# A feed-forward kernel whose second projection changes from eight block products to seven for most pairs of tiles, with the blocks of tokens in another order

## The chip, the cores and the metric

One Trainium2 chip, one of its cores. The metric is the device time of one execution in microseconds (us), as the median of the runs shown. The engines are named as the profile names them: PE is TensorE's matrix multiply and PEld its weight load, DVE is VectorE, ACT is ScalarE, POOL is GpSimd, SP is SyncE, which issues most of the DMAs.

## The reference, cut to what matters

One layer of a streaming encoder for 2048 frames of a new stream and 64 frames of a running one. A token mixer comes first (windowed attention and a spatial gate), then a normalisation, and then the part that the change is about:

```python
def _post(x, mix, ln1_g, ln1_b, w_gate_up, w_down, ln2_g, ln2_b):
    h = _layernorm(ALPHA * x + mix, ln1_g, ln1_b)
    gu = h @ w_gate_up
    f = (jax.nn.silu(gu[..., :D_FF]) * gu[..., D_FF:]) @ w_down
    return _layernorm(ALPHA * h + f, ln2_g, ln2_b)
```

The model width is 1024 and `D_FF` is 2816, which is 22 tiles of 128 features. Everything is float32.

## The kernel before

**Precision.** A float32 product is made of three matmuls in the type `fp32r`. `split` makes a high part (a copy on ACT, line 108) and a low part (a subtraction on DVE, or on POOL where the caller says so, line 109) of each operand, and PE multiplies high by high, high by low and low by high.

**Stages.** The token mixer comes first. Then `m2_load`, `m2_split`, `m2_mm`, `m2_add`, `m2_ln` and `m2_T` make the hidden rows of each tile of 128 tokens and store them, transposed, in DRAM (`h_d`). Tile 16 holds the 64 frames of the running stream. The feed-forward part goes over four blocks of tokens, of 512, 512, 512 and 576 tokens (`TB`), so the last block has five tiles.

**First projection.** For each block `b` and each of the 22 feature tiles `i`, `product(b, i, p)` makes seven products `p` in place of eight (a scheme of Winograd's kind). Each is 12 matmuls with half of the block's tokens as columns (256, or 288 in the last block). Products 1, 6, 7 and 4 collect in a PSUM bank A, 2 in B, 5 and 3 in C. ACT copies the partial sums out of A (line 859), DVE adds them up (lines 863, 866 and 877), ACT applies the silu (lines 881 and 888), and `out` multiplies and splits the result `f` of half a block (`sh`) into the tile `ff`. The order on PE is 1 of tile i, 4 and 3 of tile i-1, then 5, 6, 2, 7 of tile i, which makes 14 products for a pair of feature tiles.

**Second projection.** `down(b, c, t, h)` is one unit: six matmuls of 512 columns that multiply the pair `c` of feature tiles (2c and 2c+1) of token tile `t` by half `h` of the columns of `w_down`. DVE then adds the PSUM bank to the running sum `y` (line 1218). A pair has eight units in a block of four token tiles. The weights are loaded by SP into `draw` (line 1200, three buffers) and split into `wd` (five buffers).

**Order.** Each engine works through its instructions in the order in which the code issues them, and that order is written by hand. `order` lists the products. The main loop issues, for each position in it, the weights' forms that are due five positions later (`make`), then the product with all its work on ACT, DVE and POOL, and then what `todo` holds for that position: weight splits and units. The positions of a pair are counted from `p0`, the position of product 3 of its second feature tile. On a block's last pair the rows are finished (`finish_steps`), and the last block ends in `z_mm` and what follows, which take its last four feature tiles at once.

Of the kernel before, what the change touches and what calls it, by code (L numbers as in the profile page):

```python
# [43 lines left out]
def hybrid_step(ctx: ExitStack, tc: tile.TileContext, x_prompt, x_sample, xT_prompt, xT_sample, cache_kT, cache_v, w_in,  # L44
# [616 lines left out]
    def m2_T(t):  # L661
# [3 lines left out]
        if t == NT - 1:  # L665
            hT = f1.tile([P, KD, DEC], F32, name="hT", tag="hraw", bufs=4)
        for h in range(2):
            pt = ps1.tile([P, 4, P], F32, name="hTp", tag="pj")
            for j in range(4):
                k = 4 * h + j  # L670
                nc.tensor.transpose(pt[:, j, :m], tt[:m, k * P:(k + 1) * P], ident[:m, :m])
            nc.scalar.activation(hT[:, 4 * h:4 * h + 4, :m], pt[:, :, :m], AF.Copy, scale=1.0 / ALPHA)
        b = min(t // 4, NB - 1)
        o = (t - 4 * b) * P
        nc.scalar.dma_start(out=h_d[b][:, :, o:o + m], in_=hT[:, :, :m])
# [159 lines left out]
    ff, acc, part = {}, {}, {}  # L835
# [6 lines left out]
    def product(b, i, prod):  # L842
        n = TB[b] // 2
        w, h = wf.pop((b, i, prod)), forms[b, prod]
        bank = {1: "A", 6: "A", 7: "A", 4: "A", 2: "B", 5: "C", 3: "C"}[prod]
# [293 lines left out]
    m2_mm(13, 1)  # L1139
    m2_add(13, 1)  # L1140
    m2_T(12)
    m2_mm(13, 0)
    m2_add(13, 0)
    m2_ln(13)
    m2_load(15)
    m2_split(15)
    sums(0, 0)
    m2_mm(14, 0)
    m2_mm(14, 1)
    m2_load(16)  # L1150
    m2_split(16)
    m2_add(14, 1)
    m2_add(14, 0)
    m2_ln(14)
    m2_mm(15, 0)
    m2_T(13)
    m2_add(15, 0)
# [7 lines left out]
    m2_T(14)
    m2_add(16, 0)
    m2_mm(16, 1)
    m2_add(16, 1)
    m2_ln(16)
# [8 lines left out]
    m2_T(16)  # L1178
# [30 lines left out]
    def down(b, c, t, h, last=False):  # L1209

        m, o = rows(t), (t - 4 * b) * P
        units[0] += 1
        on_x = units[0] % 3 == 0
        pd = ps1.tile([P, 512], F32, name="pd", tag="x" if on_x else "pj", bufs=6 if on_x else 2)
        mm3(pd[:m], [((ff[b, i][:, 0, o:o + m], ff[b, i][:, 1, o:o + m]), (wd[b, i, h][:, 0], wd[b, i, h][:, 1]))
                     for i in (2 * c, 2 * c + 1)])
# [263 lines left out]
```

## Time and profile before

| what | value |
|---|---|
| median of 3 runs | 2186.51 us (2185.06 to 2187.17) |
| the profiled execution: time | 2185.13 us |
| the profiled execution: span | 2183.3 us |
| granted TensorE clock, mean | 0.989 |
| PE busy | 2109.5 us, 97% of the span |
| DVE busy | 1484.2 us, 68% |
| ACT busy | 943.1 us, 43% |
| POOL busy | 570.5 us, 26% |

The span runs from the first to the last instruction of the profiled execution; its time is 1.8 us longer. Busy times are averages over stages that differ: the token mixer and the normalisation take about the first 700 us, the four blocks of the feed-forward part the rest. Matmuls are pipelined and the profile's duration of one reaches into the next, so the cost of a matmul is read from the distance between starts.

### The profile page before, as it was taken

What the parts mean: (1) busy time and instruction counts of PE and PEld (TensorE: products, weight loads), DVE (VectorE), ACT (ScalarE), POOL (GpSimd) and SP (SyncE); (2) the same over time, 40 slices, a digit from 0 to 9 for tenths busy, and PEclk for the clock granted to TensorE, in tenths of its full rate; (3) what the DMA queues carried; (4) which work ended last, traced back from release to release, by engine and by line L of the source; (5) the groups of instructions that cost most, each with busy time, mean ns of one, the idle gap of its engine ahead of it and who ended that gap; (6) DMA issues with size and microseconds to landing.
All of it is one profiled execution on the core that took longest, in us unless ns stands there. A gap on an engine that the chain in (4) does not pass through costs nothing.

```text
span 2183.3 us, 35663 instructions
## 1 busy us (share of the span) xinstructions
PE 2109.5 (97%) x13219; PEld 1890.2 (87%) x13219; DVE 1484.2 (68%) x2899; ACT 943.1 (43%) x2255; POOL 570.5 (26%) x508
## 2 busy tenths in 40 slices
PE   8999999989998899999999999999999999999998
PEld 6888888867877899999989999989999998999996
DVE  6877777786788787887765555675555576444446
ACT  6666666663343444444433333433333343333333
POOL 0222222231122556665212221121221121111110
PEclk9999999989999899999999999999999999999999
DMA  5111111042664776777777677786777777555552
GB/s 198 39 40 39 40 39 39 27 161 102 206 215 155 281 248 240 286 251 254 279 260 250 233 258 235 264 288 194 273 248 230 239 260 241 191 191 188 192 194 92
DMA packets 172942, 418.27 MB, mean 192 GB/s; under 512 B 20800, under 2 KB 51264, under 8 KB 172768
## 3 DMA queue, kind: packets, MB, share of 16 engines
q1 hardware_dynamic: 152240, 397.31, 53.2%
q10 hardware_dynamic: 20352, 18.35, 2.5%
q8 instruction: 104, 1.70, 0.3%
q14 instruction: 70, 0.57, 0.1%
q0 software_dynamic: 176, 0.33, 0.1%
HBM read 328.31 MB, written 87.62 MB: 191 GB/s over the span
## 4 chain that ended last, share of the span: by engine, by line
PE 76%; DVE 14%; ACT 4%; issue 3%; DMA 2%; POOL 1%; SPq 0%; ACTq 0%; DVEq 0%; POOLq 0%
PE accA L853 7%; PE accA L855 7%; PE accA L854 7%; PE pd L154 7%; PE pd L155 7%; PE pd L156 7%; PE accC L854 4%; PE accC L853 4%; PE accC L855 4%; PE pj L156 2%; PE pj L155 2%; PE pj L154 2%; PE po L154 2%; PE po L156 2%; PE po L155 2%
## 5 line engine op out<-in xcount | busy, mean ns | idle before, releaser
L109 POOL TENSOR_TENSOR wf<-guraw,wf 128x512 fp32r<-128x512 f32 x173 | 249.3, 1441 | 812.0 <-ACT wf L108 742.4
L853 PE MATMUL accA<-hf,wf 128*128 128x256 f32 (+1 forms) x1408 | 407.6, 290 | 17.5 <-ACT a L859 14.6
L855 PE MATMUL accA<-hf,wf 128*128 128x256 f32 (+1 forms) x1408 | 404.9, 288 | 0.8 <-DVE wf L109 0.8
L854 PE MATMUL accA<-hf,wf 128*128 128x256 f32 (+1 forms) x1408 | 402.7, 286 | 0.0
L1218 DVE TENSOR_TENSOR y<-pd,y 128x512 f32<-128x512 f32 (+1 forms) x354 | 242.9, 686 | 163.0 <-PE pd L156 161.5
L853 PEld LDWEIGHTS accA<-hf,wf 128*128 128x128 f32 x1408 | 266.7, 189 | 29.5 <-ACT a L859 18.5
L154 PE MATMUL pd<-wd,ff 128*128 128x512 f32 (+1 forms) x708 | 280.9, 397 | 0.0
L155 PE MATMUL pd<-wd,ff 128*128 128x512 f32 (+1 forms) x708 | 280.5, 396 | 0.0
L156 PE MATMUL pd<-wd,ff 128*128 128x512 f32 (+1 forms) x708 | 279.4, 395 | 0.0
L854 PEld LDWEIGHTS accA<-hf,wf 128*128 128x128 f32 x1408 | 267.9, 190 | 8.1
L855 PEld LDWEIGHTS accA<-hf,wf 128*128 128x128 f32 x1408 | 266.7, 189 | 1.3 <-DVE wf L109 1.3
L109 DVE TENSOR_TENSOR wd<-draw,wd 128x512 fp32r<-128x512 f32 x176 | 172.4, 980 | 53.2 <-ACT wd L108 47.7
L854 PE MATMUL accC<-hf,wf 128*128 128x256 f32 (+1 forms) x704 | 201.8, 287 | 2.1 <-DVE hf L109 2.1
L853 PE MATMUL accC<-hf,wf 128*128 128x256 f32 (+1 forms) x704 | 203.5, 289 | 0.3 <-ACT hf L108 0.3
L859 ACT COPY a<-accA 128x256 f32<-128x256 f32 (+1 forms) x264 | 99.6, 377 | 239.7 <-PE accA L855 237.3
L855 PE MATMUL accC<-hf,wf 128*128 128x256 f32 (+1 forms) x704 | 202.4, 288 | 0.0
L108 ACT CAST ff<-a 128x256 fp32r<-128x256 f32 (+1 forms) x176 | 72.7, 413 | 292.8 <-DVE a L866 288.2
L108 ACT CAST wf<-guraw 128x512 fp32r<-128x512 f32 x264 | 163.2, 618 | 8.6 <-PE po L156 2.9
L156 PEld LDWEIGHTS pd<-wd,ff 128*128 128x128 f32 (+1 forms) x708 | 131.7, 186 | 33.7
L154 PEld LDWEIGHTS pd<-wd,ff 128*128 128x128 f32 (+1 forms) x708 | 131.9, 186 | 18.1
L155 PEld LDWEIGHTS pd<-wd,ff 128*128 128x128 f32 (+1 forms) x708 | 132.1, 187 | 16.3
L109 DVE TENSOR_TENSOR ff<-a,ff 128x256 fp32r<-128x256 f32 (+1 forms) x176 | 88.4, 502 | 84.6 <-ACT ff L108 84.6
(275 smaller groups left out, 4816.8 us busy)
## 6 DMA issues: line engine op xcount, KB each, us to landing
wf<-wf_d SPq DMA_DIRECT2D x264, 512.0 KB, 4.6
guraw<-in_w_gate_up_dram SPq DMA_DIRECT2D x110, 512.0 KB, 6.3
wf_d<-wf SPq DMA_DIRECT2D x88, 512.0 KB, 5.1
draw<-in_w_down_dram SPq DMA_DIRECT2D x176, 256.0 KB, 4.8
guraw<-in_w_gate_up_dram SPq DMA_DIRECT2D x66, 256.0 KB, 6.5
hraw<-h_d SPq DMA_DIRECT2D x36, 256.0 KB, 5.6
x<-in_xT_prompt_dram SPq DMA_DIRECT2D x32, 256.0 KB, 3.1
catx<-cat_d SPq DMA_DIRECT2D x16, 512.0 KB, 3.7
```

Source lines behind the costliest of these rows:

```text
L108: nc.scalar.copy(hi, src)
L109: (on or nc.vector).tensor_tensor(out=lo, in0=src, in1=hi.bitcast(F32), op=ALU.subtract)
L154: nc.tensor.matmul(out, ah, bh, start=(i == 0), stop=False)
L155: nc.tensor.matmul(out, ah, bl, start=False, stop=False)
L156: nc.tensor.matmul(out, al, bh, start=False, stop=(i == n - 1))
L853: nc.tensor.matmul(ps, wh, hh, start=(new and k == 0), stop=False, skip_group_check=not new)
L854: nc.tensor.matmul(ps, wh, hl, start=False, stop=False, skip_group_check=not new)
L855: nc.tensor.matmul(ps, wl, hh, start=False, stop=(k == 3), skip_group_check=not new)
L859: nc.scalar.copy(part[i, key][:, :n], ps)
L1218: nc.vector.tensor_tensor(out=y, in0=pd[:m], in1=y, op=ALU.add)
```

## The change

1. The block of 576 tokens is now the first block (`TB`, `TILES`), and the order of the tiles in the stage before follows it (`TSEQ`): 0, 1, 2, 3, 16, 4, and so on to 15. The last tile's transposed rows go out in two halves.
2. While the first block runs, POOL makes four sums of quarter blocks of `w_down` for each pair (`w_sum`, 44 in all), and SP stores them in DRAM (`w_store` to `wt_d`).
3. In blocks 1, 2 and 3, the pairs that `strassen(b, i)` names (2 to 9 in blocks 1 and 2, 2 to 8 in block 3, 23 pairs together) use seven products of two units each in place of eight units. A unit is now three matmuls of 512 columns and one addition to `y` on DVE. The seven weights are loaded and split one by one (`load_f`, `split_f`), and seven forms of `f` are split: three directly from the products (`put_f`), four from sums that POOL makes (`f_sums`).
4. In blocks 1 to 3 the PSUM banks have fixed roles (`bank`): A0, A1, C0, C1, S1 (which also holds product 2 of the first projection), S0, D0, D1.
5. The positions of loads, splits and units are set anew, and the last block now ends on four tiles.

```diff
-TB = (512, 512, 512, 576)
-NHX = TB[-1] // 2
-TILES = tuple(tuple(range(4 * b, 4 * b + (5 if b == NB - 1 else 4))) for b in range(NB))
+TB = (576, 512, 512, 512)
+NHX = TB[0] // 2
+TILES = tuple(tuple(range(4 * b, 4 * b + 4)) + ((NP,) if b == 0 else ()) for b in range(NB))
+
+TSEQ = sum(TILES, ())
...
-        if t == NT - 1:
-            hT = f1.tile([P, KD, DEC], F32, name="hT", tag="hraw", bufs=4)
+        if t == TSEQ[-1]:
+            hT = [f1.tile([P, 4, P], F32, name="hT", tag="hraw", bufs=4) for _ in range(2)]
...
+    def bank(name):
+
+        if name not in banks:
+            banks[name] = ps1.tile([P, 512], F32, name=f"bank{name}", **({"tag": "pj"} if name[0] == "D" else {"tag": "x", "bufs": 6}))
+        return banks[name]
+
+    def half_form():
+
+        if not spare:
+            f = f2.tile([P, 4 * NHX], F32R, name="ff", tag="ff", bufs=4)
+            spare.extend(f[:, j * 2 * NHX:j * 2 * NHX + 512].rearrange("p (s t) -> p s t", s=2) for j in range(2))
+        return spare.pop(0)
...
+    def strassen(b, i):
+
+        return b > 0 and 1 < i // 2 < NFF // 2 - (2 if b == NB - 1 else 1)
+
+    def put_f(b, c, prod, src):
+        f = ffs[b, c, prod] = half_form()
+        split(f[:, 0], f[:, 1], src)
+
+    def f_sums(b, c):
+
+        x, y = g_t.pop((b, 2 * c)), g_t.pop((b, 2 * c + 1))
+        for prod, o, a, d, op in ((5, y[:, 1], x[:, 1], y[:, 1], ALU.add), (7, x[:, 1], x[:, 0], x[:, 1], ALU.subtract),
+                                  (6, x[:, 0], y[:, 1], x[:, 0], ALU.subtract), (3, y[:, 0], y[:, 0], x[:, 0], ALU.subtract)):
+            nc.gpsimd.tensor_tensor(out=o, in0=a, in1=d, op=op)
+        for prod, o in ((5, y[:, 1]), (6, x[:, 0]), (7, x[:, 1]), (3, y[:, 0])):
+            put_f(b, c, prod, o)
...
+            acc[i, bk] = (bank({"A": f"A{i % 2}", "C": f"C{i % 2}", "B": "S1"}[bk]) if b else
+                          ps1.tile([P, 512], F32, name=f"acc{bk}", tag="x", bufs=6))
...
         def out(sh, g, u):
+            if strassen(b, i):
+                if sh == 0:
+                    g_t[b, i] = f2.tile([P, 4, P], F32, name="g", tag="wsum", bufs=3).rearrange("p (s a) q -> p s (a q)", s=2)
+                to = g_t[b, i][:, sh]
+                nc.vector.tensor_tensor(out=to, in0=u, in1=g, op=ALU.mult)
+
+                if not (sh and i % 2 == 0):
+                    put_f(b, i // 2, 4 if sh else 1 + i % 2, to)
+                if sh and i % 2:
+                    f_sums(b, i // 2)
+                return
             nc.vector.tensor_tensor(out=g, in0=u, in1=g, op=ALU.mult)
...
+    def w_sum(c, j):
+
+        i0, i1 = 2 * c, 2 * c + 1
+        out, x, y = (((i0, 0), (i0, 1), (i0, 0)), ((i0, 1), (i1, 1), (i0, 1)), ((i1, 1), (i1, 1), (i0, 0)),
+                     ((i1, 0), (i1, 0), (i1, 1)))[j]
+        nc.gpsimd.tensor_tensor(out=w_kept[out], in0=w_kept[x], in1=w_kept[y], op=ALU.subtract)
+
+    def w_store(c, j):
+        nc.sync.dma_start(out=wt_d[c][:, j], in_=w_kept[((2 * c, 0), (2 * c, 1), (2 * c + 1, 1), (2 * c + 1, 0))[j]])
...
+    def unit(b, c, prod, u):
+        pd = bank({1: f"D{u}", 6: f"D{u}", 7: f"D{u}", 4: f"D{u}", 2: "S0"}.get(prod, f"S{1 - u}"))
+        f, w = ffs[b, c, prod], wd[b, c, "f", prod]
+        new = prod in (1, 2, 5)
+        fh, fl = f[:, 0, u * P:u * P + P], f[:, 1, u * P:u * P + P]
+        nc.tensor.matmul(pd, fh, w[:, 0], start=new, stop=False, skip_group_check=not new)
+        nc.tensor.matmul(pd, fh, w[:, 1], start=False, stop=False, skip_group_check=not new)
+        nc.tensor.matmul(pd, fl, w[:, 0], start=False, stop=True, skip_group_check=not new)
+        r, h = Y_OF[prod]
+        y = y_t[TILES[b][2 * r + u]][:, h * 512:(h + 1) * 512]
+        nc.vector.tensor_tensor(out=y, in0=pd, in1=y, op=ALU.add)
...
+            if strassen(b, 2 * c):
+                for prod, q0, q1 in ((1, -7, -3), (2, -6, -2), (6, -2, 2), (5, -1, 3), (3, 1, 5), (7, 3, 7), (4, 5, 9)):
+                    at(p0 + q0, lambda b=b, c=c, prod=prod: load_f(b, c, prod))
+                    at(p0 + q1, lambda b=b, c=c, prod=prod: split_f(b, c, prod))
+                for q, prod, u in ((0, 1, 0), (1, 2, 0), (2, 1, 1), (3, 2, 1), (5, 6, 0), (6, 5, 0), (7, 5, 1), (8, 3, 0), (8, 6, 1),
+                                   (9, 3, 1), (10, 7, 0), (11, 7, 1), (12, 4, 0), (13, 4, 1)):
+                    at(p0 + q, lambda b=b, c=c, prod=prod, u=u: unit(b, c, prod, u))
+                continue
+            if b == 0:
+                d_load, d_split = (-6, -2, 8, 0), (1, 0, 10, 3)
+                for j, q0, q1 in ((0, 2, 4), (1, 4, 6), (2, 5, 7), (3, 11, 13)):
+                    at(p0 + q0, lambda c=c, j=j: w_sum(c, j))
+                    at(p0 + q1, lambda c=c, j=j: w_store(c, j))
...
-                where = (2, 3, 4, 5, 7, 8, 9, 10, 12, 13) if last else (2, 4, 5, 7, 9, 10, 12, 13)
+                where = (5, 6, 7, 8, 9, 12, 13, 14, 15, 16) if b == 0 else (2, 4, 5, 7, 9, 10, 12, 13)
                 if c == 0 and b:
-                    where = (6, 10, 12, 14, 15, 16, 17, 18, 19, 20) if last else (6, 10, 12, 14, 15, 16, 17, 18)
-                elif c == 1 and last:
-                    where = (3, 4, 5, 6, 7, 9, 10, 11, 12, 13)
+                    where = (10, 12, 14, 16, 17, 18, 19, 19) if b == 1 else (6, 10, 12, 14, 15, 16, 17, 18)
...
-    for k in range(5):
+    for k in range(4):
```

## Rows read from the trace of the kernel before

**Rows 1.** The page, busy time, share of the span and instructions of each engine.
```profile
PE 2109.5 (97%) x13219; PEld 1890.2 (87%) x13219; DVE 1484.2 (68%) x2899; ACT 943.1 (43%) x2255; POOL 570.5 (26%) x508
```

**Rows 2.** Busy time of each engine by stretch, then granted clock, DMA share, GB/s.
```profile
700.00:750.00 50.00, 41.60 (x272) 38.10 (x271) 37.06 (x46) 20.73 (x44) 24.43 (x17) 0.86 0.83 296
...
900.00:1000.00 100.00, 100.00 (x694) 93.23 (x694) 80.53 (x116) 46.27 (x102) 60.93 (x43) 1.00 0.70 249
...
1300.00:1400.00 100.00, 100.00 (x689) 92.96 (x687) 53.22 (x92) 34.82 (x79) 15.91 (x12) 1.00 0.69 232
```

**Rows 3.** Waits of PE from 740 us on: total, times, longest.
```profile
PE accA L853 <- ACT a L859: 13.2, 13, 2.8
```

**Rows 4.** PE's instructions in order of time, a pair in block 2.
```profile
1301.44 0.40 PE L154 MATMUL pd<-wd,ff 128*128 128x512 f32 x1
...
1302.84 0.28 PE L853 MATMUL accB<-hf,wf 128*128 128x256 f32 x1
...
1304.28 0.40 PE L154 MATMUL pd<-wd,ff 128*128 128x512 f32 x1
...
1334.20 0.28 PE L853 MATMUL accB<-hf,wf 128*128 128x256 f32 x1
```

**Rows 5.** DVE's instructions in order of time, the same pair.
```profile
1304.48 0.42 DVE L863 TENSOR_TENSOR a<-accB,a 128x256 f32<-128x256 f32 x1 [0.75 <-PE accB L855]
...
1315.36 0.41 DVE L863 TENSOR_TENSOR a<-accC,a 128x256 f32<-128x256 f32 x1
1316.25 0.43 DVE L866 TENSOR_TENSOR a<-a,a 128x256 f32<-128x256 f32 x1 [0.48 <-ACT a L888]
1317.15 0.43 DVE L109 TENSOR_TENSOR ff<-a,ff 128x256 fp32r<-128x256 f32 x1 [0.47 <-ACT ff L108]
```

**Rows 6.** ACT's instructions in order of time, the copy in front of that last row.
```profile
1316.71 0.41 ACT L108 CAST ff<-a 128x256 fp32r<-128x256 f32 x1 [0.49 <-DVE a L866]
```

**Rows 7.** POOL's groups of instructions by shape: count, busy, mean ns.
```profile
L109 POOL TENSOR_TENSOR xl<-x,xh 128x256 fp32r<-128x256 f32 x2 | 1.5, 729 | 0.0
```

**Rows 8.** Timeline of block 0, DVE and POOL instructions.
```profile
904.10 0.68 DVE L109 TENSOR_TENSOR wf<-wsum,wf 128x512 fp32r<-128x512 f32 x1
904.71 0.68 DVE L1218 TENSOR_TENSOR y<-pd,y 128x512 f32<-128x512 f32 x1
904.86 1.29 POOL L809 TENSOR_TENSOR wsum<-guraw 128x512 f32<-128x512 f32 x1 [1.57 <-DVE wf L109]
```

**Rows 9.** PE, the end of a unit in block 2.
```profile
1329.68 0.40 PE L156 MATMUL pd<-wd,ff 128*128 128x512 f32 x1
1329.92 0.28 PE L853 MATMUL accC<-hf,wf 128*128 128x256 f32 x1
```

**Rows 10.** DVE, the same moments.
```profile
1329.63 0.69 DVE L866 TENSOR_TENSOR a<-a,a 128x256 f32<-128x256 f32 x1 [0.48 <-ACT a L888]
1330.79 0.42 DVE L109 TENSOR_TENSOR ff<-a,ff 128x256 fp32r<-128x256 f32 x1 [0.47 <-ACT ff L108]
1331.13 0.68 DVE L1218 TENSOR_TENSOR y<-pd,y 128x512 f32<-128x512 f32 x1
```

**Rows 11.** A DVE and a POOL instruction that overlap in block 2.
```profile
1313.58 1.30 POOL L109 TENSOR_TENSOR wf<-guraw,wf 128x512 fp32r<-128x512 f32 x1 [3.48 <-ACT wf L108]
...
1313.61 1.83 DVE L109 TENSOR_TENSOR wd<-draw,wd 128x512 fp32r<-128x512 f32 x1
```

**Rows 12.** A wait of PE for DVE at a block's start.
```profile
1067.21 0.68 DVE L109 TENSOR_TENSOR hf<-hraw,hf 128x512 fp32r<-128x512 f32 x1
...
1067.94 0.39 PE L854 MATMUL accC<-hf,wf 128*128 128x256 f32 x1 [0.49 <-DVE hf L109]
```

**Rows 13.** PE's long waits at two block boundaries.
```profile
1451.78 0.39 PE L853 MATMUL accA<-hf,wf 128*128 128x256 f32 x1 [2.84 <-ACT a L859]
...
1805.72 0.40 PE L853 MATMUL accA<-hf,wf 128*128 128x288 f32 x1 [2.26 <-ACT a L859]
```

**Rows 14.** Stretches after those two waits; third column from the right: granted clock.
```profile
1454.00:1455.00 1.00, 1.00 (x4) 0.81 (x3) 1.00 (x1) 0.00 (x0) 0.85 (x1) 0.50 1.01 414
...
1805.00:1810.00 5.00, 4.28 (x28) 4.03 (x29) 4.94 (x7) 1.49 (x4) 3.25 (x2) 1.00 0.98 380
```

**Rows 15.** DMAs of `draw` in blocks 1 to 3, from issue to landing.
```profile
DMA to landing us min/median/max: 2.7/5.2/9.6
```

More of the change, by code (lines that the diff above doesn't have):

```diff
@@ L69, in hybrid_step @@
     hy_d = [dram.tile([P, D], F32, name=f"hy_d{t}") for t in range(NT)]
+    wt_d = [dram.tile([P, 4, 512], F32, name=f"wt_d{c}") for c in range(NFF // 2)]
     hs_d = [{p: dram.tile([P, 4, TB[b] // 2], F32, name=f"hs_d{b}_{p}") for p in (4, 5, 6, 7)} for b in range(NB)]
@@ L664, in m2_T @@
         hT = cat_t[t][:, 0].rearrange("p (k q) -> p k q", q=P)
-        if t == NT - 1:
-            hT = f1.tile([P, KD, DEC], F32, name="hT", tag="hraw", bufs=4)
+        if t == TSEQ[-1]:
+            hT = [f1.tile([P, 4, P], F32, name="hT", tag="hraw", bufs=4) for _ in range(2)]
+        b = next(i for i in range(NB) if t in TILES[i])
+        o = TILES[b].index(t) * P
         for h in range(2):
@@ L671, in m2_T @@
                 nc.tensor.transpose(pt[:, j, :m], tt[:m, k * P:(k + 1) * P], ident[:m, :m])
[L672 to L675, printed above, removed]
+            half = hT[h] if t == TSEQ[-1] else hT[:, 4 * h:4 * h + 4]
+            nc.scalar.activation(half[:, :, :m], pt[:, :, :m], AF.Copy, scale=1.0 / ALPHA)
+            if t == TSEQ[-1]:
+                nc.scalar.dma_start(out=h_d[b][:, 4 * h:4 * h + 4, o:o + m], in_=half[:, :, :m])
+        if t != TSEQ[-1]:
+            nc.scalar.dma_start(out=h_d[b][:, :, o:o + m], in_=hT[:, :, :m])
         nc.scalar.dma_start(out=hy_d[t][:m], in_=tt[:m])
@@ L833, in form, with ff_tile @@
             nc.gpsimd.tensor_tensor(out=src, in0=gu_src[b, i][2], in1=src, op=ALU.subtract)
-    ff, acc, part = {}, {}, {}
+    ff, acc, part, banks = {}, {}, {}, {}
+    ffs, spare, g_t = {}, [], {}
+    def bank(name):
[7 more added lines that the diff above has]
+        return spare.pop(0)
+    def ff_tile(b, i, k):
+        m = rows(TILES[b][k])
+        if b == 0:
+            return tuple(ff[b, i][:, s_, k * P:k * P + m] for s_ in range(2))
+        return tuple(ff[b, i, k // 2][:, s_, k % 2 * P:k % 2 * P + m] for s_ in range(2))
+    def strassen(b, i):
[10 more added lines that the diff above has]
+            put_f(b, c, prod, o)
     def tmp(name):
@@ L1138, in hybrid_step @@
     sources(0, 1)
[L1139 to L1146, printed above, removed]
-    sums(0, 0)
[L1148 to L1157, printed above, removed]
+    m2_mm(TSEQ[13], 1)
+    m2_add(TSEQ[13], 1)
+    m2_T(TSEQ[12])
+    m2_mm(TSEQ[13], 0)
+    m2_add(TSEQ[13], 0)
+    m2_ln(TSEQ[13])
+    m2_load(TSEQ[15])
+    m2_split(TSEQ[15])
+    sums(0, 0)
+    m2_mm(TSEQ[14], 0)
+    m2_mm(TSEQ[14], 1)
+    m2_load(TSEQ[16])
+    m2_split(TSEQ[16])
+    m2_add(TSEQ[14], 1)
+    m2_add(TSEQ[14], 0)
+    m2_ln(TSEQ[14])
+    m2_mm(TSEQ[15], 0)
+    m2_T(TSEQ[13])
+    m2_add(TSEQ[15], 0)
     make(2)
-    m2_mm(15, 1)
-    m2_add(15, 1)
-    m2_ln(15)
+    m2_mm(TSEQ[15], 1)
+    m2_add(TSEQ[15], 1)
+    m2_ln(TSEQ[15])
     make(3)
-    m2_mm(16, 0)
+    m2_mm(TSEQ[16], 0)
     make(EARLY - 1)
[L1165 to L1169, printed above, removed]
+    m2_T(TSEQ[14])
+    m2_add(TSEQ[16], 0)
+    m2_mm(TSEQ[16], 1)
+    m2_add(TSEQ[16], 1)
+    m2_ln(TSEQ[16])
     store_forms(0)
     product(*order[0])
-    m2_T(15)
+    m2_T(TSEQ[15])
     sums(0, 1, (5, 6))
@@ L1177, in hybrid_step @@
     prep.pop(0)()
-    m2_T(16)
+    m2_T(TSEQ[16])
     product(*order[3])
@@ L1209, in down @@
     def down(b, c, t, h, last=False):
-        m, o = rows(t), (t - 4 * b) * P
+        m, k = rows(t), TILES[b].index(t)
         units[0] += 1
[L1213 to L1216, printed above, removed]
+        if b:
+            pd = bank(("D0", "D1", "S0")[units[0] % 3])
+        else:
+            on_x = units[0] % 3 == 0 and c < NFF // 2 - 1
+            pd = ps1.tile([P, 512], F32, name="pd", tag="x" if on_x else "pj", bufs=6 if on_x else 2)
+        mm3(pd[:m], [(ff_tile(b, i, k), (wd[b, i, h][:, 0], wd[b, i, h][:, 1])) for i in (2 * c, 2 * c + 1)])
         y = y_t[t][:m, h * 512:(h + 1) * 512]
@@ L1333, in hybrid_step @@
     NO = len(order) // NB
-    for t in TILES[0]:
-        at(6 + t, lambda t=t: new_y(t))
+    for k, t in enumerate(TILES[0]):
+        at(6 + k, lambda t=t: new_y(t))
     for b in range(NB):
```

89 lines of the change are left out of this document (54 added, 35 removed).

## The prediction

> **What bounds the kernel now.** First the page's busy times: PE is busy 97% of the span, DVE 68%, POOL 26% [rows 1]. These are averages, so next the same columns by stretch. From 900 to 1000 us (block 0) and from 1300 to 1400 us (block 2) PE is busy all 100 us at the full clock, with DVE at 80.5 and 53.2 us; from 700 to 750 us, where the feed-forward part begins, PE is busy 41.6 of 50 us and the clock is 0.86 [rows 2]. The waits say the same: from 740 us on PE waits 13.2 us for ACT's copies, in 13 pieces [rows 3], which lie at the block boundaries, and next to nothing inside a block. So inside a block PE sets the time, and a matmul saved there is time saved, unless something else becomes late.
>
> **What a matmul costs.** The timeline of PE shows a unit's six matmuls from 1301.44 to 1302.84, so 1.40 us, 0.233 us each, and a product's twelve to 1304.28, so 1.44 us; from one product 2 to that of the next pair it is 1334.20 - 1302.84 = 31.36 us [rows 4]. That is 14 x 1.44 + 8 x 1.40 = 31.36: no idle time at all.
>
> **Matmuls removed.** A changed pair has 7 products x 2 units x 3 = 42 matmuls of 512 columns in place of 8 x 6 = 48. Six fewer give 6 x 0.233 = 1.40 us, and 23 pairs 32.2 us. The 576-token block changes places, which leaves all other counts as they are.
>
> **Work added in a changed pair.** DVE gets 14 additions to y in place of 8, and three more low parts each of f and of the weights. A 512-column instruction takes 0.68 us and hands DVE on after 0.61 [rows 8], so a 256-column one of 0.42 hands it on after about 0.34. That is 9 x 0.61 + 3 x 0.34 = 6.5 us, on top of 0.532 x 31.36 = 16.7 us: 23.2 of about 31 us, 75%. Block 0 ran DVE at 80.5% without a wait of PE [rows 2], so the load alone costs nothing. ACT gets six short copies (34.8% busy now), POOL four additions of 128x256, SP three more loads. What matters is the order on DVE.
>
> **The new chain.** At p0, `product` issues product 3, then `f_sums`, and only then does `todo` issue the first units. DVE's queue then reads: add product 3, multiply, low part of form 4, low parts of forms 5, 6, 7 and 3 (each waits for POOL and ACT), addition of unit (1,0), low part of the weights for product 4, addition of unit (2,0). Unit (2,1) uses the same bank S0 as (2,0), so PE can't start it before that last addition is done. DVE does wait in order: at 1329.92 a unit was done [rows 9], DVE sat idle 0.47 us for ACT, did the low part at 1330.79, and only then, at 1331.13, the addition of that unit [rows 10].
>
> From T, the end of product 3's matmuls:
> - DVE's addition starts 0.20 later (1304.28 to 1304.48) [rows 4, 5]. The multiplication starts 0.89 after that, the low part of form 4 0.90 later again and takes 0.43 [rows 5]: T + 2.42.
> - POOL starts 0.08 after DVE's result (904.78 to 904.86) [rows 8]. An addition of 128x256 takes 0.73 [rows 7]; four of them, one after the other, with 0.03 of overlap, take 2.83: T + 5.33.
> - ACT's copy starts some 0.05 later, and DVE's low part 0.44 after the copy's start (1316.71 to 1317.15) [rows 5, 6]: T + 5.82.
> - That low part hands DVE on after 0.34, the addition of (1,0) after 0.61, the weights' low part after 0.61, and the addition of (2,0) takes 0.68: T + 8.06. PE follows 0.05 after DVE (1067.89 to 1067.94) [rows 12]: T + 8.11.
>
> PE itself would be there after unit, product 5, unit, product 6, unit, product 2: 3 x 0.70 + 3 x 1.44 = T + 6.42. It waits 1.69 us.
>
> Collisions add to it. A DVE instruction with two inputs in SBUF that meets a POOL instruction waits for it: 1.83 us in place of 0.68, ending 0.56 after POOL's end [rows 11]. The low parts of forms 5 and 6 meet POOL's additions so; I allow 0.1 to 0.2 us and take 1.75 us for the wait. Its lower bound is 1.4 (POOL at 0.65), its upper bound 2.6 (each collision delays POOL by a whole low part). Per pair the change then saves 1.40 and loses 1.75; 23 x 1.75 = 40.3 us, bounds 32 to 60.
>
> A rule of the Trainium skill speaks against this part: the GPSIMD Engine Reference, section Engine selection, keeps two-input elementwise work off GpSimd, as about two times slower than VectorE. By that an addition would take an estimated 0.84 us in place of the row's 0.73 [rows 7], and the sum would come out 23 x 4 x 0.11 = 10 us higher.
>
> **Block 0.** POOL makes 44 more sums of 128x512 at 1.29 us [rows 8], 5.2 us per pair. There it is busy 60.9% of 31.36 us = 19.1 us [rows 2], so 24.3 us of a pair that grows longer (ten units and wider products): hidden, by a five-position lead of the forms. If that cover went, a pair would lose one sum, 1.3 us. The stores and loads of SP cost nothing while a load's four-position lead (4 x 2.24 = 9 us) covers its landing, 5.2 us at the median and 9.6 at most [rows 15].
>
> **The first stage and the boundaries.** Block 0's forms and products get 12.5% wider in the stretch where PE already idles [rows 2]: of 37 us of DVE time there perhaps a third scales, 37 x 0.33 x 0.125 = 1.5 us, the wider last tile adds about 0.5, and the fifth tile's finishing at the first boundary about 1. I take +3 us. Tile 16 now comes fifth, so its load follows close behind the store of its rows by the mixer; its split comes a loop step later, which hides it. Fixed banks and new positions could also close some of the 13.2 us of waits [rows 3], so the bounds are -6 and +12.
>
> **The sum.** 2185.1 (the profiled execution's time: 2183.3 of span and 1.8 around it) - 32.2 + 40.3 + 3 = 2196.2 us. The profiled execution lies 1.4 us below the median of the runs, well within the 0.2% (4.4 us) that a measurement of this kernel can tell from no change.
>
> **The rivals.**
> - *Most likely, 0.50:* the wait at unit (2,1), 1.4 to 2.4 us in each changed pair: 2187 to 2212, 2196 taken. 0.40 of it is slower, 0.10 within the bound.
> - *Faster, 0.20:* the wait isn't there, because DVE comes to the additions in time. What speaks for it is DVE's and ACT's free time; what speaks against it is the order [rows 9, 10]. It decides where the wait falls under (32.2 - 3)/23 = 1.27 us. With none: 2185.1 - 32.2 + 3 = 2156.
> - *A shorter chain, 0.12:* POOL and DVE hand over faster than rows of other shapes say, wait about 1.0 us: 2185.1 - 32.2 + 23 + 3 = 2179; half of it faster, half within the bound.
> - *Slow sums on POOL, 0.08:* additions that take twice DVE's 0.42 us [rows 5], so 0.84 us, make the chain 0.44 us longer in each pair: 2196 + 10 = 2206. The Trainium skill's section on engine selection, above, has it so.
> - *The clock, 0.05:* after PE's wait of 2.84 us at a boundary the granted clock fell to 0.50, its lower level of 1.2 GHz; after one of 2.26 us it stayed at 1.00 [rows 13, 14]. Some 3.4 us at half the rate lose 1.7 us. If the new wait came near 2.8 us in every pair, the time would be about 2185 - 32 + 23 x (2.8 + 1.7) + 3 = 2260. [...]
> - *Late weights, 0.05:* seven loads in place of four raise the DMA share (0.69 in block 2) [rows 2]. A load that lands at 9.6 us instead of 5.2 is 0.6 us late, and ACT, DVE and PE wait: up to 23 x 0.6 = 14 us more, 2210.
>
> **The numbers.** Faster: 0.20 + 0.06 = 0.26. Within the bound: 0.10 + 0.06 = 0.16. Slower: 0.40 + 0.08 + 0.05 + 0.05 = 0.58. The range goes from 2158, which leaves out about half of the case without a wait, to 2220, which takes in slow sums and late weights and leaves out the clock and the upper end of the wait. Of the likeliest case alone it is 2187 to 2212.
>
> **What would show it.** Right: in the middle of blocks 1 to 3, PE waits once per pair, 1.4 to 2.4 us, at the second unit of product 2, put down to DVE's addition to y; DVE idles for ACT or POOL just before its additions; a pair takes 31.4 to 32.4 us where eight units took 31.36; block 0 takes about 36.7 us per pair (14 products of 1.44 x 1.125 us and 10 units of 1.40) with no waits. Wrong: a pair of 29.96 us with PE fully busy (the faster rival), half-clock stretches inside blocks (the clock), PE waiting for weight splits behind a DMA (late weights), or waits in block 0 behind POOL's sums.

## The result and the profile after

The changed kernel takes 2257.93 us (median of 4, 2257.21 to 2258.49), the kernel before 2186.10 us beside it; the ratio is 1.0328, with a 95% interval of 1.031 to 1.0346. It is slower by 3.3%, outside the predicted range of 2158 to 2220 us.

The page of the changed kernel, its span and the busy times, answers to [rows 1]:
```profile
span 2256.3 us, 36282 instructions
...
PE 2111.6 (94%) x13081; PEld 1887.1 (84%) x13081; DVE 1613.2 (71%) x3176; ACT 1001.6 (44%) x2385; POOL 697.8 (31%) x644
```
138 matmuls fewer (23 x 6) than in [rows 1], yet PE is busy 2.1 us longer. So besides waits something makes PE work more slowly. The waits of PE from 700 us on, total, times and longest, show the first part:
```profile
PE bankS L1321 <- DVE y L1326: 58.1, 25, 5.7
PE bankA L900 <- ACT a L906: 14.8, 8, 4.7
...
PE bankS L900 <- DVE y L1326: 2.9, 4, 1.2
```
Nothing like the first row is in [rows 3]. L1321 is the first matmul of `unit`, L1326 its addition to y. It is the wait that the prediction put at unit (2,1), in each of the 23 pairs. One of them, in the last block, on DVE, then POOL, then PE; the number in brackets is the idle time ahead of an instruction and what ended it:
```profile
2037.20 0.42 DVE L910 TENSOR_TENSOR a<-bankC,a 128x256 f32<-128x256 f32 x1 [0.20 <-PE bankC L902]
2038.11 0.43 DVE L917 TENSOR_TENSOR g<-a,a 128x256 f32<-128x256 f32 x1 [0.48 <-ACT a L949]
2039.01 0.42 DVE L113 TENSOR_TENSOR ff<-g,ff 128x256 fp32r<-128x256 f32 x1 [0.47 <-ACT ff L112]
2040.72 0.63 DVE L113 TENSOR_TENSOR ff<-g,ff 128x256 fp32r<-128x256 f32 x1 [1.29 <-ACT ff L112]
2042.43 1.30 DVE L113 TENSOR_TENSOR ff<-g,ff 128x256 fp32r<-128x256 f32 x3 [1.08 <-ACT ff L112]
2043.66 0.68 DVE L1326 TENSOR_TENSOR y<-bankD,y 128x512 f32<-128x512 f32 x1
2044.26 0.68 DVE L113 TENSOR_TENSOR wf<-guraw,wf 128x512 fp32r<-128x512 f32 x1
2044.86 0.68 DVE L1326 TENSOR_TENSOR y<-bankS,y 128x512 f32<-128x512 f32 x1
```
```profile
2039.52 3.27 POOL L879 TENSOR_TENSOR g<-g 128x256 f32<-128x256 f32 x4 [1.69 <-DVE ff L113]
...
2039.52 0.74 POOL L879 TENSOR_TENSOR g<-g 128x256 f32<-128x256 f32 x1 [1.69 <-DVE ff L113]
2040.33 0.74 POOL L879 TENSOR_TENSOR g<-g 128x256 f32<-128x256 f32 x1
...
2042.04 0.75 POOL L879 TENSOR_TENSOR g<-g 128x256 f32<-128x256 f32 x1
```
```profile
2043.27 0.28 PE L902 MATMUL bankS<-hf,wf 128*128 128x256 f32 x1
2045.59 0.50 PE L1321 MATMUL bankS<-wd,ff 128*128 128x512 f32 x1 [2.05 <-DVE y L1326]
```
DVE stands idle 1.29 and 1.08 us for the splits of the sums, with two additions to y behind them that have long been possible; the second of these frees S0. With T = 2037.00 (the end of product 3: the addition's start at 2037.20 less the prediction's 0.20 us), the steps came at T + 1.11, 2.01 and 2.52 (POOL), as worked out (1.09, 1.99, 2.50). From there they fell behind: POOL took 3.27 us for its four additions (the first row; the others show three of them singly) instead of 2.83, and PE went on at T + 8.59 instead of 8.11. The additions themselves take 0.74 us, near the 0.73 that were expected. But the second begins 0.81 us after the first, so 0.07 after its end, where the sum let them overlap by 0.03.

The second part is the clock. Here are PE's rows at the product 2 of three pairs that follow one another, and the same wait in the second of them (the first has the wait just shown):
```profile
2041.96 0.28 PE L900 MATMUL bankS<-hf,wf 128*128 128x256 f32 x1
...
2075.54 0.28 PE L900 MATMUL bankS<-hf,wf 128*128 128x256 f32 x1
...
2079.17 0.50 PE L1321 MATMUL bankS<-wd,ff 128*128 128x512 f32 x1 [2.05 <-DVE y L1326]
...
2107.61 0.28 PE L900 MATMUL bankS<-hf,wf 128*128 128x256 f32 x1
```
The first pair takes 33.58 us, the second 32.07, both with a wait of 2.05. The stretches behind the two waits (columns as in [rows 2]) tell them apart by the granted clock, the third column from the right:
```profile
2046.00:2048.00 2.00, 2.00 (x13) 1.91 (x12) 1.07 (x3) 0.90 (x2) 0.00 (x0) 0.73 0.34 92
2048.00:2050.00 2.00, 2.00 (x11) 2.00 (x11) 1.62 (x3) 0.92 (x3) 0.27 (x1) 0.50 0.77 207
2050.00:2052.00 2.00, 2.00 (x15) 1.88 (x14) 0.13 (x1) 0.89 (x2) 1.01 (x1) 0.92 0.99 383
...
2080.00:2082.00 2.00, 2.00 (x19) 2.00 (x18) 1.00 (x3) 1.32 (x4) 0.00 (x0) 1.00 0.41 102
2082.00:2084.00 2.00, 2.00 (x17) 1.87 (x16) 1.34 (x4) 1.37 (x3) 1.29 (x1) 1.00 0.88 309
```
After the first wait the clock went to its lower level, 1.2 GHz; after the second it stayed at 2.4. PE is busy either way, so this loss shows in no wait: 11 matmuls in 2 us instead of 17 to 19. By their lengths, and by the granted clock, 18 of the 23 pairs have such a fall: 13 of the 18 with a wait of 2.04 to 2.05 us, and all five of those that come next.

The third part is what the prediction had not looked at. In five pairs of blocks 1 and 2 the wait at unit (2,1) is longer, 3.1 to 5.7 us. In four of them POOL makes sums of the next block's h (the hidden rows, of which the first projection's products 5, 6, 7 and 4 need sums). The longest, on POOL, then DVE, then PE:
```profile
1699.08 3.23 POOL L879 TENSOR_TENSOR g<-g 128x256 f32<-128x256 f32 x4 [1.26 <-DVE ff L113]
1702.27 1.45 POOL L747 TENSOR_TENSOR hsum<-hraw 128x512 f32<-128x512 f32 x1
1703.80 1.32 POOL L747 TENSOR_TENSOR hsum<-hraw,hsum 128x512 f32<-128x512 f32 x1
```
```profile
1701.97 3.43 DVE L113 TENSOR_TENSOR ff<-g,ff 128x256 fp32r<-128x256 f32 x3 [1.06 <-ACT ff L112]
```
```profile
1707.73 0.79 PE L1321 MATMUL bankS<-wd,ff 128*128 128x512 f32 x1 [5.74 <-DVE y L1326]
```
POOL goes straight on to the sums of h (`later_steps`, L747), and DVE's three low parts, 1.30 us in the other pair, take 3.43 us beside them: the collision of [rows 11] again. The fifth pair, with a wait of 3.18 us, has no sum of h beside it. There ACT waits for a raw weight tile of the first projection; POOL's low part of a weight form comes late with it and falls beside DVE's multiplication, which takes 1.31 us in place of 0.43, so the whole chain starts late. ACT, POOL, DVE, PE:
```profile
1284.05 0.62 ACT L112 CAST wf<-guraw 128x512 fp32r<-128x512 f32 x1 [1.49 <-DMA guraw<-in_w_gate_up_dram]
```
```profile
1284.75 1.30 POOL L113 TENSOR_TENSOR wf<-guraw,wf 128x512 fp32r<-128x512 f32 x1 [4.13 <-ACT wf L112]
```
```profile
1285.03 1.31 DVE L917 TENSOR_TENSOR g<-a,a 128x256 f32<-128x256 f32 x1 [0.78 <-ACT a L949]
```
```profile
1293.34 0.80 PE L1321 MATMUL bankS<-wd,ff 128*128 128x512 f32 x1 [3.18 <-DVE y L1326]
```
The two longest waits have this late load as well (ACT waits 0.96 and 1.45 us). Why the load is late isn't shown; in spread_alone (experiment 5), which moves the sums of h and their stores, all 23 waits are 2.03 to 2.05 us.

### The profile page after: what moved, and what is told of

It is laid out like the page before. It is cut to its first block, busy times and chain, and to the rows that moved or that the text cites. A ratio compares the mean times of both kernels' runs of the same rounds, so it can differ in the third digit from the quotient of the medians.

```text
span 2256.3 us, 36282 instructions
## 1 busy us (share of the span) xinstructions
PE 2111.6 (94%) x13081; PEld 1887.1 (84%) x13081; DVE 1613.2 (71%) x3176; ACT 1001.6 (44%) x2385; POOL 697.8 (31%) x644
## 4 chain that ended last, share of the span: by engine, by line
PE 59%; DVE 21%; ACT 6%; issue 5%; POOL 4%; DMA 4%; ACTq 0%; SPq 0%; DVEq 0%; POOLq 0%
PE bankA L900 5%; PE bankA L901 4%; PE bankA L902 4%; POOL g L879 2%; PE pj L158 2%; PE pj L159 2%; PE pj L160 2%; DVE ff L113 2%; PE po L160 2%; PE po L158 2%; PE po L159 2%; DVE y L1326 2%; PE pd L159 2%; PE bankC L901 2%; PE pd L160 2%
## 5 line engine op out<-in xcount | busy, mean ns | idle before, releaser
L900 PE MATMUL bankA<-hf,wf 128*128 128x256 f32 x1056 | 312.7, 296 | 14.9 <-ACT a L906 14.8
L901 PE MATMUL bankA<-hf,wf 128*128 128x256 f32 x1056 | 310.6, 294 | 0.0
L902 PE MATMUL bankA<-hf,wf 128*128 128x256 f32 x1056 | 310.4, 294 | 0.0
L900 PEld LDWEIGHTS bankA<-hf,wf 128*128 128x128 f32 x1056 | 213.5, 202 | 27.5 <-ACT a L906 18.3
L901 PEld LDWEIGHTS bankA<-hf,wf 128*128 128x128 f32 x1056 | 213.1, 202 | 9.4
L902 PEld LDWEIGHTS bankA<-hf,wf 128*128 128x128 f32 x1056 | 212.7, 201 | 0.0
L906 ACT COPY a<-bankA 128x256 f32<-128x256 f32 x198 | 73.3, 370 | 203.6 <-PE bankA L902 203.3
L901 PE MATMUL bankC<-hf,wf 128*128 128x256 f32 x528 | 149.3, 283 | 2.7 <-DVE hf L113 2.7
L112 ACT CAST wd<-draw 128x512 fp32r<-128x512 f32 x245 | 150.8, 616 | 1.5 <-PE bankD L160 0.8
L900 PE MATMUL bankC<-hf,wf 128*128 128x256 f32 x528 | 149.4, 283 | 0.0
L902 PE MATMUL bankC<-hf,wf 128*128 128x256 f32 x528 | 148.4, 281 | 0.0
L113 DVE TENSOR_TENSOR ff<-g,ff 128x256 fp32r<-128x256 f32 x161 | 80.2, 520 | 86.9 <-ACT ff L112 86.9
L1326 DVE TENSOR_TENSOR y<-bankD,y 128x512 f32<-128x512 f32 x184 | 125.8, 684 | 22.5 <-PE bankD L1323 22.5
L112 ACT CAST ff<-g 128x256 fp32r<-128x256 f32 x161 | 63.2, 406 | 163.5 <-DVE g L917 101.2
L900 PE MATMUL accA<-hf,wf 128*128 128x288 f32 x352 | 105.0, 298 | 8.5 <-ACT a L906 4.9
L1321 PE MATMUL bankS<-wd,ff 128*128 128x512 f32 x138 | 58.4, 423 | 58.1 <-DVE y L1326 58.1
L901 PEld LDWEIGHTS bankC<-hf,wf 128*128 128x128 f32 x528 | 99.5, 188 | 8.7 <-DVE hf L113 3.2
L902 PE MATMUL accA<-hf,wf 128*128 128x288 f32 x352 | 104.0, 296 | 0.4 <-DVE wf L113 0.4
```

The costliest lines, as they stand in the source:

```text
L112: nc.scalar.copy(hi, src)
L113: (on or nc.vector).tensor_tensor(out=lo, in0=src, in1=hi.bitcast(F32), op=ALU.subtract)
L900: nc.tensor.matmul(ps, wh, hh, start=(new and k == 0), stop=False, skip_group_check=not new)
L901: nc.tensor.matmul(ps, wh, hl, start=False, stop=False, skip_group_check=not new)
L902: nc.tensor.matmul(ps, wl, hh, start=False, stop=(k == 3), skip_group_check=not new)
L906: nc.scalar.copy(part[i, key][:, :n], ps)
```

## The experiments

All kernels are the changed kernel with the edit shown, cut to what matters. Times are medians; ratios, with a 95% interval, are to the kernel before, run beside them.

**1. late_forms: the splits out of the chain's way.**
```
@@ f_sums
-        for prod, o in ((5, y[:, 1]), (6, x[:, 0]), (7, x[:, 1]), (3, y[:, 0])):
-            put_f(b, c, prod, o)
+        late_f[b, c] = {5: y[:, 1], 6: x[:, 0], 7: x[:, 1], 3: y[:, 0]}
@@ behind the list of units
+                for q, prod in ((3, 6), (4, 5), (5, 7), (5, 3)):
+                    at(p0 + q, lambda b=b, c=c, prod=prod: put_f(b, c, prod, late_f[b, c][prod]))
```


> GpSimd's four sums stay where they are; the splits of their results move behind the wait's place, from the last product 3 of the pair to the third, fourth and fifth product after it. Theory (VectorE, in order, stands before the four low parts until GpSimd has summed, so that the eviction of the first unit of product 2 and with it the second unit are late): the wait of 2.0 us at that unit goes from the 23 pairs, and with it the falls of the clock; a pair takes 30.0 to 30.5 us instead of 32.1 or 33.6, the time is about 2168 us (2160 to 2180). Rival 1 (VectorE and GpSimd have too much to do on their shared port, whatever the order): the wait comes back at the units of products 6, 5 or 3, and the time stays above 2230 us. Rival 2 (a late weight form or draw lies beside it): the wait stays at the same unit with another releaser, and the time stays within 1% of 2258 us.

Measured: 2188.87 us, ratio 1.001 (1.0 to 1.0019). The same work in another order on DVE and ACT gives back 69 us. Two neighbouring product 2 in its trace:
```profile
1381.57 0.28 PE L899 MATMUL bankS<-hf,wf 128*128 128x256 f32 x1
...
1411.33 0.28 PE L899 MATMUL bankS<-hf,wf 128*128 128x256 f32 x1
```
29.76 us: no wait at unit (2,1) and no fall of the clock, as the theory said, and rivals 1 and 2 fall. But the time is 21 us over the theory's. Four pairs stayed long, by 2.5, 8.8, 2.6 and 6.7 us, all with sums of h; the two in which the next block's forms are split took 31.9 and 31.6 us.

**2. unit21_later and unit21_earlier: the length of the wait.**
```
-                ... (2, 1, 1), (3, 2, 1), (5, 6, 0) ...
+                ... (2, 1, 1), (4, 2, 1), (5, 6, 0) ...     (later)
+                ... (2, 1, 1), (2, 2, 1), (5, 6, 0) ...     (earlier)
```


> Only the second unit of product 2 moves, by one product of 1.44 us. Theory (one late eviction, at a fixed moment after the pair's last product 3): the wait of 2.05 us shrinks to about 0.6 us, the clock does not fall any more behind it, a pair takes about 30.7 us and the time is about 2258 - 23 x 1.44 - 30 = 2195 us (2188 to 2210). If the clock falls whatever the wait's length: 2258 - 33 = 2225 us. Rival (VectorE is late by its load, not by one chain): the wait moves with the unit and stays near 2 us, the time within 0.5% of 2258 us.

> The kernel of the change with only the second unit of product 2 moved the other way, one product of 1.44 us earlier. Theory (one late eviction at a fixed moment): the wait grows from 2.05 to about 3.5 us in all 23 pairs. If the clock then falls behind every wait for the same 3.4 us: 2258 + 23 x 1.44 + 5 x 1.5 = 2299 us, pairs of about 35.0 us. If a longer wait makes a longer fall, as the waits of 3.4 to 6.0 us in the kernel of the change did (6.8 us at the lower level, 1.7 us more in each pair): about 2335 us, pairs of about 36.7 us. If the clock were no part of the cost: 2291 us.

Measured: 2208.45 us later (ratio 1.0097, 1.0082 to 1.0112), 2301.4 us earlier (1.0526, 1.0507 to 1.0546). The moment of the eviction is fixed, and PE's waiting follows from when it gets there: earlier, the wait is 3.44 us in the last block; later, PE stands 0.52 us at another place (for ACT's copy out of A) and pairs with neither h sums nor the next block's splits take mostly 30.6 to 30.8 us (two take 31.1 and 31.8), with no fall of the clock. Earlier, six such pairs in the last block take 34.8 to 35.7 us, 35.35 on average, where the wait alone (3.83 us from one matmul's start to the next's, instead of 0.12) would make 33.5: a fall then costs 1.9 us on average, not much more than behind a wait of 2.05 us (1.5). The total is that of the equal fall, but the falls aren't equal: in two of the six pairs the lower clock lasts 6.8 us instead of 3.4, and part of that lies in PE's wait. In the changed kernel, too, falls of 6.8 us came behind only three of the five longer waits.

**3. sums_on_dve: a shorter chain, more work on DVE.**
```
-            nc.gpsimd.tensor_tensor(out=o, in0=a, in1=d, op=op)
+            nc.vector.tensor_tensor(out=o, in0=a, in1=d, op=op)
```


> The four sums of each pair are made by VectorE itself, in front of the same four splits. Theory (the length of the chain to the eviction sets the wait): four additions of about 0.42 us take 1.7 us instead of 3.3 us on GpSimd, with no handing over and no collision, and the wait falls by about 1.0 to 1.5 us to 0.5 to 1.0 us; the clock falls in few pairs: about 2258 - 23 x 1.2 - 25 = 2205 us (2190 to 2220). Rival (VectorE's own amount of work is what makes it late): 1.7 us more of it in each pair lengthen the wait by as much, 2258 + 23 x 1.7 = 2297 us.

Measured: 2209.82 us, ratio 1.01 (1.0085 to 1.0115). DVE does four more additions in each pair and the kernel is 48 us faster: DVE was late by waiting, not by load. In the last block the wait is 0.93 us, the clock stays up and a pair takes 30.97 us.

**4. no_strassen and no_w_sums: the change without its pairs.**
```
@@ strassen
-        return b > 0 and 1 < i // 2 < NFF // 2 - (2 if b == NB - 1 else 1)
+        return False
@@ no_w_sums, besides
-                for j, q0, q1 in ((0, 2, 4), (1, 4, 6), (2, 5, 7), (3, 11, 13)):
+                for j, q0, q1 in ():
```


> The second projection of all pairs goes by eight products as before; the order of the blocks, the fixed banks and the weight sums of the first block (then never read) stay. Theory (the pairs by seven products cost 59 us net of the 73 us that were lost; the rest, 14 us, is the start of the stage, the first block with its weight sums, the boundaries and the end): about 2186 + 14 = 2200 us (2194 to 2206). Rival (what is left of the loss comes from the pairs by seven products as well): 2186 us within 3 us. Rival (the blocks' order, the banks and the sums are the main cause): over 2225 us.

> As no_strassen (2192.1 us), with the first block's weight sums and their stores left out; nothing reads them there. Theory (they are hidden: the first block's steady pairs take 36.13 us with them, as the block of 576 tokens took in the kernel before without them): 2192 us within 2 us, and the 5 us over the kernel before belong to the order of the blocks. Rival (they cost what is left): 2187 us within 1.5 us.

Measured: 2192.14 us (ratio 1.0024, 1.0013 to 1.0035) and 2190.08 us (1.0018, 1.0008 to 1.0027). So the order of the blocks with its fixed banks costs some 4 us. For the weight sums 2 us are left, and the intervals overlap: they are hidden, or nearly. In the middle of block 0 two stretches of no_strassen, each from the product 2 of a pair to that of the next, take 36.47 and 37.30 us; the others there, and these two in no_w_sums, take the steady 36.13. no_strassen came 2 us under its range: of the 14 us that the theory put beside the pairs only 5 to 7 belong to the order and the weight sums; experiment 6 and the table below have the others.

**5. spread_alone, late_stores, late_spread: the sums of h.** late_stores and late_spread have the edit of late_forms too.
```
@@ later_steps: the store leaves sub
-            nc.sync.dma_start(out=hs_d[b][prod][:, 2 * kk:2 * kk + 2], in_=t[out, kk])
+        def store(out, kk, prod):
+            nc.sync.dma_start(out=hs_d[b][prod][:, 2 * kk:2 * kk + 2], in_=t[out, kk])
@@ late_stores
+            for d, out, prod in ((10, "t1", 5), (12, "t2", 6), (14, "b12", 7), (16, "b21", 4)):
+                yield q + d, lambda kk=kk, out=out, prod=prod: store(out, kk, prod)
@@ spread_alone and late_spread (stores three positions after the sums)
-            q = -100 + 24 * kk
+            q = -132 + 48 * kk
+            subs = (-118, -104, -90, -89) if kk == 0 else (-76, -62, -48, -47)
```


> The kernel of the change as it is, with the h sums and their stores spread as in late_spread, and nothing else. Theory: only the pairs with h sums shrink, from 35.7, 35.9, 37.8, 36.1 and 37.9 us to the 32.1 or 33.6 us of the others; the wait of about 2.05 us stays in all 23 pairs and the clock goes on falling behind most of them: 2258 - 14 = 2244 us (2238 to 2250). Rival (the crowding of GpSimd's h sums is the main cause of the whole loss): below 2215 us.

> As late_forms (2188.9 us), but the four stores of the next block's h sums are issued four positions after the sums that they store, so that SyncE's queue need not stand behind GpSimd; the sums stay where they are. In late_forms four pairs by seven products are still long, by 2.5, 8.8, 2.5 and 6.7 us over 29.77 us, all where GpSimd makes h sums. Theory A (the store waits for GpSimd in SyncE's queue, and the draws and weight forms behind it come late): the pairs that were long by 8.8 and 6.7 us become short, the time is about 2176 us (2172 to 2180). Theory B (the h sums delay GpSimd's other work and slow VectorE on the shared port; the stores are harmless): 2189 us within 3 us.

> As late_forms with the stores behind as in late_stores, and the eight h sums of the next block spread over the block, mostly one for each pair, eight positions after the pair's last product 3, instead of four in a row in two pairs. If the h sums' crowding is the whole rest of late_forms' loss in these blocks: four pairs shrink by 20.5 us together, about 2168 us (2163 to 2174), which is under the kernel before. Rival (an h sum of 1.3 to 1.5 us delays VectorE wherever it stands): small waits in more pairs, 2178 to 2190 us.

Measured: 2243.39 us (ratio 1.0255, 1.024 to 1.027), 2174.34 us (0.9946, 0.9929 to 0.9962) and 2174.87 us (0.9948, 0.9933 to 0.9963). The first two came as theory and theory A had it. Spread alone, the five long pairs go and the wait of 2 us and the falls stay (17 of the 23 pairs have one): h sums are a part of the loss, not its main cause. What was left in late_forms was mostly the stores in SP's queue: a store waits there for POOL's sum, and the loads behind it wait too. SP issues nothing from 1304.1 us to the first row here, which comes as the first sum is done. SP's rows in late_forms, around the two h sums that followed f_sums in POOL's queue, and what ACT waited for later:
```profile
1317.34 0.32 SPq L748 DMA_DIRECT2D hs_d<-hsum  x1
...
1319.04 0.32 SPq L748 DMA_DIRECT2D hs_d<-hsum  x1
...
1321.17 1.04 SPq L805 DMA_DIRECT2D guraw<-in_w_gate_up_dram  x2
```
```profile
1330.61 0.62 ACT L112 CAST wf<-guraw 128x512 fp32r<-128x512 f32 x1 [4.92 <-DMA guraw<-in_w_gate_up_dram]
```
In late_stores, which is 2.8 us ahead at this pair, the same load is issued at 1313.12, so 5.2 us sooner, and no such wait follows; the pair goes from 38.6 to 32.1 us. late_spread came out 7 us over the theory and under the rival's range: no pair is longer than 31.3 us for h sums, but each sum costs 0.35 us in its pair where it is alone (30.13 us) and 1.5 us where two stand together (31.2).

**6. late_tail, one_per_pair, best.** Another loss shows in the last 14 us. A buffer holds two half forms (the split results of half a block). With an odd number of them made before, the last four feature tiles' halves share buffers across tiles, and ACT waits to write the last one until the first products of `z_mm` have read its neighbour. ACT in late_stores:
```profile
2137.36 0.42 ACT L952 ACTIVATE a<-a 128x256 f32<-128x256 f32 x1 [1.04 <-DVE a L913]
2145.74 0.41 ACT L112 CAST ff<-a 128x256 fp32r<-128x256 f32 x1 [7.97 <-PE zp L160]
```
```
@@ product, out (late_tail on late_stores; one_per_pair on late_spread)
+            if (b, i, sh) == (NB - 1, NFF - 4, 0):
+                spare.clear()
@@ one_per_pair
-            q = -132 + 48 * kk
+            q = -146 + 60 * kk
-            subs = (-118, -104, -90, -89) if kk == 0 else (-76, -62, -48, -47)
+            subs = (-132, -118, -104, -90) if kk == 0 else (-76, -62, -48, -34)
@@ best: one_per_pair, but for block 1, whose h sums fall into block 0, q and subs as in late_stores
```


> As late_stores (2174.3 us), but ahead of the last two pairs of the last block a half of a buffer that the odd number of half forms left over is dropped, so that each later tile's two halves share a buffer again. Theory (in the last block ScalarE waits 8 us to write the last tile's second half, because its buffer still holds a half that the first z products read, and the final chain on VectorE starts late): the end after the last matmul goes from 13.6 back to 10.3 us: about 2171 us (2169.5 to 2172.5). Rival (the end is longer for the draws or the order of units): 2174 us within 1 us.

> Late splits, late stores, the dropped half as in late_tail, and the eight h sums one to a pair, eight positions after its last product 3 (in late_spread a pair with one such sum took 30.13 us, with two 31.23, with none 29.77). Theory: 3.3 us less at the end and four times 1.1 - 0.36 less for the doubles than late_spread's 2174.9: about 2168.5 us (2166 to 2171), 0.8% under the kernel before. Rival (the sum in a boundary pair costs more than it gives): 2172 us or more.

> As one_per_pair (2177.9 us), but the h sums of the first later block are loaded and made at their old positions in the block of 576 tokens; the later blocks' stay one to a pair. In one_per_pair's trace the pairs by seven products are at their best (27.6 us under no_strassen's together), but one pair of the first block takes 49.0 us instead of 38.4. Theory (its loads of h, pulled ahead to the start of that block, delay it): that pair returns to 38 to 39 us, the time is about 2167 us (2165 to 2170). Rival (the long pair was an accident of that profile or comes from the later blocks' changes): 2175 us or more.

Measured: 2173.17 us (ratio 0.9938, 0.9923 to 0.9953), 2177.92 us (0.996, 0.9947 to 0.9972) and 2167.31 us (0.9911, 0.9896 to 0.9926). In late_tail the end after the last matmul went from 13.6 to 10.0 us and ACT's wait is gone, but the total gained only 1.2 us, a little short of the expected range; in its profile the first product 2 of block 0 came 3 us later than in late_stores (717.4 against 714.3 us), and why isn't settled; in best, which has the same edit, it came at 713.5. one_per_pair missed: its pairs were as good as expected, but a pair of block 0 took 49.0 us, with PE waiting 10.46 us for ACT. best put the sums of that block back, and the time came out as expected, 0.9% under the kernel before:
```profile
span 2162.6 us, 36248 instructions
...
PE 2075.8 (96%) x13081; PEld 1855.4 (86%) x13081; DVE 1626.3 (75%) x3176; ACT 994.4 (46%) x2385; POOL 704.9 (33%) x644
```
```profile
PE bankS L1325 <- DVE y L1330: 1.4, 2, 0.8
```
DVE's and POOL's work is that of the changed kernel and a little over; the wait of 58.1 us is 1.4.

## Why the prediction was wrong

The direction, the place and the cause of the wait were right; the sum was 62 us short. The clock rival's 2260 us lies 2 us from the measured time, but by luck: it took 2.8 us of wait and a fall in every pair, and no sums of h. In spans the change cost 73.0 us (2256.3 against 2183.3), where the sum had 11.1. Term by term, from the pairs' lengths:

| term | predicted | measured | from |
|---|---|---|---|
| matmuls removed | -32.2 | -36.6 | 23 x (31.36 - 29.77), late_forms |
| wait at unit (2,1) | +40.3 | +52.9 | 23 x (32.07 - 29.77); as idle time the profile has 2.05 of each 2.30 |
| clock behind it | 0 | +27.2 | 18 x (33.58 - 32.07) |
| sums of h and late loads in the way | 0 | +17.9 | rest: the 23 stretches, product 2 to product 2, are 61.4 over no_strassen's |
| first stage, block 0, boundaries | +3 | +8.3 | no_strassen's span 6.7 over before's, and 1.6 in the stretches left |
| the end | 0 | +3.3 | 13.6 against no_strassen's 10.3 us after the last matmul |

- **The step that failed** is the clock rival's condition. The prediction took from [rows 13, 14] that the clock falls behind a wait of 2.84 us and not behind one of 2.26, gave a fall in every pair only "near 2.8 us" and 0.05. The likeliest wait was already of a size at which it mostly falls here: behind 2.05 us it fell in 13 of 18 pairs (17 of 23 in spread_alone), behind 3.1 us and more in five of five, behind 0.52 and 0.93 (unit21_later, sums_on_dve) in none of the pairs that have neither h sums nor the next block's splits beside them. One row each way said that it can fall and that it can stay, and not where the border is. Nor is there one between 2.26 and 2.84 us: in no_strassen the clock stayed up behind a wait of 2.84 us at a boundary.
```profile
1509.96 0.39 PE L900 MATMUL bankA<-hf,wf 128*128 128x256 f32 x1 [2.84 <-ACT a L906]
```
```profile
1510.00:1512.00 2.00, 2.00 (x15) 1.91 (x16) 2.00 (x4) 0.70 (x2) 2.00 (x2) 1.00 1.02 396
1512.00:1514.00 2.00, 2.00 (x15) 1.84 (x14) 2.00 (x1) 0.00 (x0) 1.04 (x1) 1.00 1.02 418
```
So the length of a wait alone doesn't decide; what does stays open. The falls cost 27.2 us where the sum had nothing; the price of one was right, 1.7 us said, 1.5 measured. The Trainium skill's TensorE: Matmul & The Clock Gate, section Why this matters for your kernels, warns of PE's idle gaps between bursts of matmuls from a certain length on. The waits of 2.05 us are shorter than the length it names, and the clock fell behind most of them; the measurement decides.
- **The wait was mis-sized**, 1.75 taken, 2.30 measured, inside its bounds of 1.4 to 2.6. Most of it is POOL's chain, 0.44 us longer (3.27 against 2.83): the four additions stand 0.07 to 0.08 us apart, where the sum had an overlap of 0.03, for which it gave no row. They hang together: the second and the third overwrite an input of the one before, the fourth reads the result of the third. The trace of the kernel before had such a pair, the second addition reading the first one's result, and it stands 0.08 us apart:
```profile
896.96 1.75 POOL L809 TENSOR_TENSOR wsum<-guraw 128x512 f32<-128x512 f32 x1
898.79 1.37 POOL L809 TENSOR_TENSOR wsum<-wsum,guraw 128x512 f32<-128x512 f32 x1
```
Another 0.1 us is the first matmul behind the wait, 0.33 us to the next one's start in place of 0.23. The collisions that were feared beside it cost little in the pairs without h sums: the low part of form 5 took 0.63 us in place of 0.42.
- **Left out: POOL's other queue entries.** The sum counted POOL's additions but not what POOL had queued behind them in blocks 1 and 2. The sums of h are in the kernel before as well, and PE had no wait for them there [rows 3]. spread_alone gives 14.5 us for them with what hangs on them, the table's rest 18: 15 in the five long pairs, 3 in the two pairs where the next block's forms are split, which stay long in all variants.
- **Matmuls**: 29.77 us is 0.19 under the 29.96 that the counts give: in late_forms 11 of a pair's 14 products take 1.42 us in place of 1.44. Why they do, no run shows.
- **The first stage and boundaries** came inside their bounds. Block 0 was near: 36.13 us per steady pair against 36.7, and the weight sums hidden, or nearly.
- **The end** wasn't foreseen; the odd half form explains it (late_tail).
- **The other rivals.** The chain's lateness of 0.44 us is by chance the one that the rival of slow sums had, and 10 of the 62 us; its mechanism is out, since an addition took 0.74 us and not 0.84. Late weights did occur: in three of the five long pairs ACT waited 0.96 to 1.49 us for a raw load of the first projection, and in late_forms up to 4.92 us, behind the stores. The rival had the waiting right; its price, 0.6 us in every pair, was not what happened. By the Trainium skill's GPSIMD Engine Reference, section Engine selection, the additions belong on VectorE; sums_on_dve agrees, by 48 us, with the splits where the change has them. Moving the splits and leaving the sums on GpSimd (late_forms) gives 21 us more. Both edits together were not run, so which engine is the better place then isn't shown.

## What to carry to other kernels

When a change puts a chain through three engines, look at what else is queued in order behind each of its waits: here moving four splits from ahead of two evictions (additions out of a PSUM bank) to behind them gave back 69 us, with the sums left where they were. A short wait that repeats in every tile is to be priced with the clock behind it, even where one row of the same length shows none. And when a queue gets new work, list its old entries, POOL's and SP's both: what was harmless off the path isn't harmless beside the new.

## What was not expected of the hardware

A wait of PE of 2.05 us is followed by the lower clock in some pairs and not in others that look the same (33.58 and 32.07 us, one behind the other), and a wait of 2.84 us in no_strassen isn't. Three of DVE's low parts of 128x256, 1.30 us together in a pair without h sums, took 3.43 us beside two of POOL's 128x512 sums, which themselves took 1.45 and 1.32 us. Where the two met, DVE paid nearly all of it.
